# One decoder block on one core: planner and scheduler replaced by source order, timed pieces and one paced list of conditioning and gate

## The chip, the cores and the metric

The kernel runs on one core of a Trainium2 chip. The metric is the device time of one execution in microseconds: the median of three runs before the change is 1742.32 us (1741.33 to 1743.38).

## The reference

One layer on x of 256 tokens by 4096 channels, all float32:

```python
mod = silu(c) @ w_ada + b_ada               # c: 4096 values, w_ada: 4096 x 12288
shift, scale, gate = split(mod, 3)
h = rmsnorm(x, norm_g) * (1 + scale) + shift
p = h @ w_in                                # 4096 x 14336: a_b, a_c, a_x, a_z, b_v, b_g, b_z
y_a = a_b * conv3(a_c * a_x) * silu(a_z)    # causal depthwise, along the tokens
u = conv31(b_v * sigmoid(b_g)) + conv_b_b
y_b = silu(layernorm(u)) * silu(b_z)
out = rmsnorm(x + gate * (concat(y_a, y_b) @ w_out), final_g)
```

## The kernel before

**Products.** The activations are the stationary operand (128 channels by 128 tokens), the weights stream as 512 columns. Each float32 operand is split in a high part and a low remainder, so one block of 128 channels by 512 columns takes six matmuls (`products`, L142): three for each half of the tokens. This text calls these six a *unit*. `w_in` has 28 column tiles of 32 units (896 units), `w_out` 8 of 32 (256), 1152 in all. Weights come two units at a time, 512 KB (`load_w`, L131): a DMA on SP's queue, the high part by a cast on ScalarE (L138, tile w_h), the low part by a subtraction on VectorE (L139, tile w_l). A *step* of the program is two units; there are three buffers of each part.

**Blocks.** The 32 channel blocks are worked in six passes over all 28 column tiles (`BLOCKS`, L31), so that the first pass needs only the first blocks' activations. Between passes a tile's sum is taken out of PSUM (tile acc, L446) and put back (L438), both on ScalarE. In the last pass the tiles finish one after another, and the work on the heads starts: 31 taps of the long convolution for four groups of heads (L350: four products on ScalarE, L351: one sum on VectorE, 120 such pairs), the short convolution (`silu_gate_A`), the transposes of both on TensorE, then the layer norm (`norm_B`) and the gates of y_b while the first half of `w_out` is multiplied.

**Conditioning.** scale, shift and gate are 96 columns of 128 values, each a product of a 128 x 4096 slice of `w_ada` with silu(c), summed along the row by VectorE (`ada_steps`, L179, sum on L189): four *pieces* of 1024 columns (512 KB) for each. A channel block needs the eight pieces of its scale and shift before its activations can be made (`make_h`, L233). The 128 pieces of gate are needed only by the end of the layer.

**Order.** The source puts work at steps: `run_due` (L287) calls what a queue has due at a step; scale and shift pieces get their times from a hull over the first use of each block (L411), the gate pieces are spread evenly over 170 steps from the start of the last pass (L426, `GATE_RUN`). On top of that the tile framework's scheduler orders the instructions of each engine by its own priorities and costs. Within an engine, and on SP's DMA queue, instructions then run strictly in that order. Weights are asked for one step ahead (`AHEAD`). Seven buffers of 512 KB serve weights and pieces alike (`raws`, L92).

Of the kernel before, what the change touches and what calls it, by code (L numbers as in the profile page):

```python
# [16 lines left out]
ALU = mybir.AluOpType  # L17
# [13 lines left out]
BLOCKS = (4, 4, 4, 6, 6, 8)  # L31

EARLY = {0: 12, 1: 10}
KD = 2
AHEAD = 1
LEAD = 2
KEEP = 3
HOLD = 5
ROW = 1024
GATE_RUN = (0, 170)  # L40
A_SPAN = 5

# [42 lines left out]
def decoder_block(ctx: ExitStack, tc: tile.TileContext, x, c, w_mod, w_gate, w_in, w_out, xt, pk, final_g, out):  # L85
    nc = tc.nc
    const = ctx.enter_context(tc.tile_pool(name="const", bufs=1))
    const.tile([P, 420], F32, name="pad")
    big = ctx.enter_context(tc.tile_pool(name="big", bufs=33))
    cbc = ctx.enter_context(tc.tile_pool(name="cbc", bufs=1))  # L90
    dram = ctx.enter_context(tc.tile_pool(name="dram", bufs=1, space=bass.MemoryType.DRAM))
    raws = ctx.enter_context(tc.tile_pool(name="raws", bufs=7))  # L92
    split = ctx.enter_context(tc.tile_pool(name="split", bufs=3))
# [19 lines left out]
    pks = const.tile([P, PK], F32, name="pks")  # L113
    nc.scalar.dma_start(pks, pk)
# [6 lines left out]
    def rsqrt(y, v, t):  # L121

        nc.scalar.activation(out=t, in_=v, func=AF.Sqrt)
        nc.vector.reciprocal(out=y, in_=t)
        nc.vector.tensor_tensor(out=t, in0=y, in1=y, op=ALU.mult)
        nc.vector.tensor_tensor(out=t, in0=t, in1=v, op=ALU.mult)
        nc.vector.tensor_scalar(out=t, in0=t, scalar1=-0.5, scalar2=1.5, op0=ALU.mult, op1=ALU.add)
        nc.vector.tensor_tensor(out=y, in0=y, in1=t, op=ALU.mult)


    def load_w(src, k0, name, keep=False):  # L131
        raw = rawt(f"{name}_r")
        nc.sync.dma_start(raw, src[k0 // KD])
        if keep:
            hi, lo = (bigt(f"{name}_{t}", (P, KD, CT), F32R) for t in "hl")
        else:
            hi, lo = (split.tile([P, KD, CT], F32R, tag=t, name=f"{name}_{t}") for t in "hl")
        nc.scalar.copy(hi, raw)  # L138
        nc.vector.tensor_tensor(out=lo, in0=raw, in1=hi.bitcast(F32), op=ALU.subtract)  # L139
        return hi, lo  # L140

    def products(ps, act, parts, k0, first, last, tokens=range(NS), seeded=False):  # L142

        hi, lo = parts
        for i in range(KD):
            a = act[(k0 + i) // 2]
            f, l = first and i == 0, last and i == KD - 1
            for s in tokens:
                out = ps[s] if isinstance(ps, list) else ps[:, s]
                ah, al = (a[:, (k0 + i) % 2, h, s * P:(s + 1) * P] for h in range(2))  # L150
# [13 lines left out]
    pts = [const.tile([P, 4], F32, name=f"part{i}") for i in range(4)]  # L164
    part_no = itertools.count()
    cB = cbc.tile([P, D], F32, name="cB")
    hT = {}

    def broadcast_c():

        for q in range(D // ROW):
            row = bigt(f"crow{q}", (P, ROW))
            nc.sync.dma_start(row[:1], c[:, q * ROW:(q + 1) * ROW])
            ps = pmm.tile([P, NS, CT], F32, tag="ps", name=f"cps{q}")
            for h in range(2):
                nc.tensor.matmul(ps[:, h], ones[:1], row[:1, h * CT:(h + 1) * CT], start=True, stop=True)  # L176
            nc.scalar.activation(out=cB[:, q * ROW:(q + 1) * ROW], in_=ps, func=AF.Silu)

    def ada_steps(name, srcs, bias, dst):  # L179

        state = {}

        def step(q):
            raw = rawt(f"{name}_{q}", (P, ROW))
            nc.sync.dma_start(raw, srcs[q])
            if q == 0:
                state["part"] = pts[next(part_no) % 4]
            p = state["part"]
            nc.vector.tensor_tensor_reduce(out=raw, in0=raw, in1=cB[:, q * ROW:(q + 1) * ROW], scale=1.0, scalar=p[:, q - 1:q] if q else bias, op0=ALU.mult, op1=ALU.add, accum_out=dst if q == D // ROW - 1 else p[:, q:q + 1])  # L189

        return [lambda q=q: step(q) for q in range(D // ROW)]

    def mod_steps(k):

        def finish():
# [6 lines left out]
        return work + [finish]  # L202
# [12 lines left out]
    def gate_steps():
        work = [f for k in range(KT) for f in ada_steps(f"gate{k}", w_gate[k], pks[:, O_BGATE + k:O_BGATE + k + 1], gateT[:, k:k + 1])]
        return work + [gate_finish]


    plan = [(w_in[e], k) for _, e, k0, k1 in SEGS for k in range(k0, k1, KD)]  # L220
    end_in = len(plan)
    start_last = sum((k1 - k0) // KD for b, _, k0, k1 in SEGS if b < len(BLOCKS) - 1)
    conv_end = end_in + CONV_END
    plan += [(w_out[dt], k0 + k) for k0 in (0, KT // 2) for dt in range(NDT) for k in range(0, KT // 2, KD)]
    loaded = []
    step = 0

    def load_ahead(last):
        while len(loaded) <= min(last, len(plan) - 1):
            src, k = plan[len(loaded)]  # L230
            loaded.append(load_w(src, k, f"w{len(loaded)}", 0 <= len(loaded) - len(plan) + KT // 2 // KD < HOLD))

    def make_h(k0, n):  # L233

        if k0 + n <= 4 * len(kept):
            srcs = [kept[k // 4][:, k % 4:k % 4 + 2] for k in range(k0, k0 + n, 2)]
        else:
            xc = rawt(f"xc{k0}", (P, n, S))
            nc.sync.dma_start(xc, xt[:, k0:k0 + n])
            srcs = [xc[:, q:q + 2] for q in range(0, n, 2)]  # L240
        for q, src in enumerate(srcs):
            nc.vector.tensor_tensor(out=src, in0=src, in1=rstd.unsqueeze(1).broadcast_to([P, 2, S]), op=ALU.mult)
            for i in range(2):
                k = k0 + 2 * q + i
                nc.scalar.activation(out=src[:, i], in_=src[:, i], func=AF.Identity, scale=gscT[:, k:k + 1], bias=modT[:, k:k + 1])
            t = hT[k0 // 2 + q] = bigt(f"hT{k0 // 2 + q}", (P, 2, 2, S), F32R)
            split_act(t, src)


    kept = []  # L250

    def x_stats():

        ps = misc("x_ps", (P, S))
        for ci in range(8):
            xc = bigt(f"xs{ci}", (P, 4, S))
            nc.sync.dma_start(xc, xt[:, 4 * ci:4 * ci + 4])
            sq = xc
            if ci < KEEP:
                kept.append(xc)  # L260
                sq = bigt(f"xq{ci}", (P, 4, S))
            nc.scalar.activation(out=sq, in_=xc, func=AF.Square)
            if ci == 0:
                total = sq
            else:
                nc.vector.tensor_tensor(out=total, in0=total, in1=sq, op=ALU.add)
        for i in range(4):
            nc.tensor.matmul(ps, ones, total[:, i], start=i == 0, stop=i == 3)
        y = const.tile([P, S], F32, name="x_rstd")
        nc.vector.tensor_scalar(out=total[:, 2], in0=ps, scalar1=1.0 / D, scalar2=EPS, op0=ALU.mult, op1=ALU.add)  # L270
        rsqrt(y, total[:, 2], total[:, 3])
        return y

    broadcast_c()
    rstd = x_stats()
    first_steps = [f for k in range(KD) for f in mod_steps(k)]
    for f in first_steps[:-4]:
        f()
    load_ahead(AHEAD)
    for f in first_steps[-4:]:  # L280
        f()
# [341 lines left out]
```

## Time and profile before

| | |
|---|---|
| median of three runs | 1742.32 us |
| profiled execution, its own time | 1744.85 us |
| its span | 1743.0 us |
| TensorE busy | 1644.6 us (94%), 7073 matmuls |
| VectorE busy | 1421.8 us (82%) |
| ScalarE busy | 1163.6 us (67%) |
| DMA | 524.51 MB, mean 301 GB/s |

The busy time of TensorE is no measure of its work here: a matmul's record lasts longer than the distance to the next. What counts is the distance from one product to the next, and where it is longer than in an undisturbed stretch. The stages below are cut at products number 1, 769, 4033, 5377 and 6145 of the 6912 (units 0, 128, 672, 896 and 1024), so that the stretch between two cuts can be compared with the number of its products.

### The profile page before, as it was taken

What the parts mean: (1) busy time and instruction counts of PE and PEld (TensorE: products, weight loads), DVE (VectorE), ACT (ScalarE), POOL (GpSimd) and SP (SyncE); (2) the same over time, 40 slices, a digit from 0 to 9 for tenths busy, and PEclk for the clock granted to TensorE, in tenths of its full rate; (3) what the DMA queues carried; (4) which work ended last, traced back from release to release, by engine and by line L of the source; (5) the groups of instructions that cost most, each with busy time, mean ns of one, the idle gap of its engine ahead of it and who ended that gap; (6) DMA issues with size and microseconds to landing.
All of it is one profiled execution on the core that took longest, in us unless ns stands there. A gap on an engine that the chain in (4) does not pass through costs nothing.

```text
span 1743.0 us, 20848 instructions
## 1 busy us (share of the span) xinstructions
PE 1644.6 (94%) x7073; PEld 1323.9 (76%) x7073; DVE 1421.8 (82%) x1707; ACT 1163.6 (67%) x1558; POOL 1.0 (0%) x8
## 2 busy tenths in 40 slices
PE   4799999999999999999999999989998999999997
PEld 1577788888888888888888777766666777778885
DVE  6887777877777777787776899999999999976675
ACT  4555966577666556566556599998898777464453
POOL 0000000000000000000000000000000000000000
PEclk9999999999999999999999999999999999999999
DMA  8998999999999999999998998868887999679663
GB/s 318 319 363 322 325 328 343 321 335 326 327 317 343 330 322 320 324 342 313 333 326 308 332 304 286 300 220 273 271 266 264 314 314 320 221 273 321 201 201 149
DMA packets 146771, 524.51 MB, mean 301 GB/s; under 512 B 16196, under 2 KB 16228, under 8 KB 146664
## 3 DMA queue, kind: packets, MB, share of 16 engines
q1 hardware_dynamic: 146520, 522.81, 86.1%
q8 instruction: 55, 0.90, 0.2%
q10 hardware_dynamic: 144, 0.37, 0.1%
q14 instruction: 52, 0.43, 0.1%
HBM read 518.91 MB, written 4.21 MB: 300 GB/s over the span
## 4 chain that ended last, share of the span: by engine, by line
PE 63%; DVE 18%; issue 10%; ACT 5%; DMA 4%; DVEq 0%; ACTq 0%
PE ps L152 17%; PE ps L153 17%; PE ps L151 17%; DVE w_l L139 5%; DVE cv L351 5%; DVE gate L189 3%; PE pb L151 3%; PE pb L153 3%; PE pb L152 3%; DMA mod<-in_w_mod 2%; ACT w_h L138 2%; ACT pr L350 1%; DVE mod L189 1%; DMA gate<-in_w_gate 1%; PE cps L176 1%
## 5 line engine op out<-in xcount | busy, mean ns | idle before, releaser
L139 DVE TENSOR_TENSOR w_l<-w_r,w_h 128x1024 fp32r<-128x1024 f32 x576 | 702.7, 1226 | 236.1 <-ACT w_h L138 234.3
L138 ACT CAST w_h<-w_r 128x1024 fp32r<-128x1024 f32 x576 | 600.2, 1048 | 260.1 <-PE ps L153 140.7
L152 PE MATMUL ps<-w_l,hT 128*128 128x512 f32 x1792 | 709.4, 396 | 26.5 <-DVE w_l L139 26.3
L151 PE MATMUL ps<-w_h,hT 128*128 128x512 f32 x1792 | 703.4, 393 | 27.6 <-ACT hT L157 18.1
L153 PE MATMUL ps<-w_h,hT 128*128 128x512 f32 x1792 | 703.6, 393 | 1.1 <-DVE hT L158 1.1
L152 PEld LDWEIGHTS ps<-w_l,hT 128*128 128x128 f32 x1792 | 339.2, 189 | 115.4 <-DVE w_l L139 46.2
L151 PEld LDWEIGHTS ps<-w_h,hT 128*128 128x128 f32 x1792 | 339.5, 190 | 104.0 <-ACT hT L157 19.2
L153 PEld LDWEIGHTS ps<-w_h,hT 128*128 128x128 f32 x1792 | 339.6, 190 | 71.9 <-DVE hT L158 3.2
L446 ACT ACTIVATE acc<-ps 128x1024 f32<-128x1024 f32 x163 | 167.4, 1027 | 223.0 <-PE ps L153 222.6
L189 DVE CUSTOM_DVE_ANT_0 mod<-mod,cB,part 128x1024 f32<-128x1024 f32 x192 | 245.7, 1280 | 26.0 <-DMA mod<-in_w_mod 24.1
L350 ACT ACTIVATE pr<-uT,pks 128x255 f32<-128x255 f32 (+14 forms) x480 | 197.0, 488 | 1.8 <-DVE cv L351 1.6
L351 DVE TENSOR_TENSOR cv<-cv,pr 128x1020 f32<-128x1020 f32 (+14 forms) x120 | 140.3, 1169 | 3.6 <-ACT pr L350 3.4
L438 ACT COPY ps<-acc 128x1024 f32<-128x1024 f32 x135 | 137.0, 1016 | 0.4
L189 DVE CUSTOM_DVE_ANT_0 gate<-gate,cB,part 128x1024 f32<-128x1024 f32 x96 | 124.2, 1294 | 1.6 <-DMA gate<-in_w_gate 1.5
L152 PE MATMUL pa<-w_l,yT 128*128 128x512 f32 x256 | 104.0, 406 | 7.9 <-DVE w_l L139 7.4
L151 PE MATMUL pa<-w_h,yT 128*128 128x512 f32 x256 | 100.3, 394 | 1.8 <-ACT w_h L138 1.8
L153 PE MATMUL pa<-w_h,yT 128*128 128x512 f32 x256 | 100.9, 394 | 0.0
L151 PE MATMUL pb<-w_h,yT 128*128 128x512 f32 x256 | 99.7, 389 | 0.0
L152 PE MATMUL pb<-w_l,yT 128*128 128x512 f32 x256 | 99.6, 389 | 0.0
L153 PE MATMUL pb<-w_h,yT 128*128 128x512 f32 x256 | 99.6, 389 | 0.0
L189 DVE CUSTOM_DVE_ANT_0 mod<-mod,cB,pks 128x1024 f32<-128x1024 f32 x64 | 81.9, 1280 | 12.3 <-DMA mod<-in_w_mod 12.3
L152 PEld LDWEIGHTS pa<-w_l,yT 128*128 128x128 f32 x256 | 48.7, 190 | 27.4 <-DVE w_l L139 17.6
(122 smaller groups left out, 678.5 us busy)
## 6 DMA issues: line engine op xcount, KB each, us to landing
w_r<-in_w_in SPq DMA_DIRECT2D x448, 512.0 KB, 5.0
mod<-in_w_mod SPq DMA_DIRECT2D x256, 512.0 KB, 5.1
gate<-in_w_gate SPq DMA_DIRECT2D x128, 512.0 KB, 4.6
w_r<-in_w_out SPq DMA_DIRECT2D x128, 512.0 KB, 4.6
xs<-in_xt SPq DMA_DIRECT2D x8, 512.0 KB, 10.0
xr<-in_x SPq DMA_DIRECT2D x8, 512.0 KB, 6.7
out<-o SPq DMA_DIRECT2D x16, 256.0 KB, 2.9
xc<-in_xt SPq DMA_DIRECT2D x10, 256.0 KB, 4.6
```

The costliest lines, as they stand in the source:

```text
L138: nc.scalar.copy(hi, raw)
L139: nc.vector.tensor_tensor(out=lo, in0=raw, in1=hi.bitcast(F32), op=ALU.subtract)
L151: nc.tensor.matmul(out, ah, hi[:, i], start=f, stop=False, skip_group_check=seeded)
L152: nc.tensor.matmul(out, ah, lo[:, i], start=False, stop=False, skip_group_check=seeded)
L153: nc.tensor.matmul(out, al, hi[:, i], start=False, stop=l, skip_group_check=seeded)
L176: nc.tensor.matmul(ps[:, h], ones[:1], row[:1, h * CT:(h + 1) * CT], start=True, stop=True)
L189: nc.vector.tensor_tensor_reduce(out=raw, in0=raw, in1=cB[:, q * ROW:(q + 1) * ROW], scale=1.0, scalar=p[:, q - 1:q] if q else bias, op0=A ...
L350: nc.scalar.activation(out=pr[:, j, sh:], in_=u[:, j, :S - sh], func=AF.Copy, scale=cbw[:, 4 * i + j, TAPS - 1 - sh:TAPS - sh])
L351: nc.vector.tensor_tensor(out=o[:, :, sh:], in0=o[:, :, sh:], in1=pr[:, :, sh:], op=ALU.add)
L438: nc.scalar.copy(ps, acc[e])
L446: nc.scalar.activation(out=acc[e], in_=ps, func=AF.Silu if k1 == KT and e >= 24 else AF.Copy)
```

## The change

- `tc.manual_schedule()`: the scheduler no longer orders anything; each engine runs in source order. The work beside the products is cut into one-engine pieces which the source puts at set units (`put`).
- Weights are asked for two steps ahead, in four buffers of their own; conditioning pieces are 2048 columns (1 MB), two for a column, in three buffers of their own.
- One list (`filler`) holds the pieces of scale and shift in the order of their use, and behind them all of gate. `run_due` takes the next one when a running account of VectorE's time and of the DMA's (at `RATE`, 0.385 MB per us) says that it fits, or when it is due.
- The first pass is two blocks; 15 of its tiles do the first block alone (`ALONE`), so one column of conditioning precedes the first product instead of two. The statistics of x are taken from x by ScalarE's row sums (L354) rather than by sums of squares on VectorE.
- In the second half of `w_out` the first half's sum is put back into PSUM by ScalarE (`seed_b`) instead of being added by VectorE. The gate's column goes to DRAM from ScalarE's queue.

```diff
-BLOCKS = (4, 4, 4, 6, 6, 8)
-EARLY = {0: 12, 1: 10}
+BLOCKS = (2, 4, 4, 6, 8, 8)
+ALONE = 15
+EARLY = {1: 14}
-AHEAD = 1
+AHEAD = 2
+ROW = 2048
...
+UNIT = 1.363
+FIRST = 29.0
+RATE = 0.385
+W_LOAD = 0.2622
+ADA_LOAD = 1.0486
+LOW_PART = 0.57
+ADA_SUM = 2.42
+SLACK = 3.0
...
+            if b == 0 and n < ALONE:
+                k1 = 1
...
+    def run_due():
+
+        nonlocal vec, load
+        t = FIRST + UNIT * now
+        while queue and queue[0][0] <= now:
+            _, cost, f = queue.pop(0)
+            vec = max(vec, t - SLACK) + cost
+            f()
+        while filler:
+            due, mb, cost, f = filler[0]
+            if due > now and (max(vec, t - SLACK) + cost > t + UNIT * KD or max(load, t - SLACK) + mb / RATE > t + UNIT):
+                break
+            filler.pop(0)
+            vec = max(vec, t - SLACK) + cost
+            load = max(load, t - SLACK) + mb / RATE
+            f()
...
+    work = [f for k in range(1, KT) for f in mod_steps(k)]
+    gates_due = end_in + KT // 2 * NDT - 20
+    need = [(FIRST_USE[k] - H_DUE, len(work) * k // (KT - 1)) for k in range(1, KT)]
+    work += gate_steps()
...
+    for n, f in enumerate(work):
+        filler.append((float(np.interp(n + 1, [d for _, d in hull], [t for t, _ in hull])), ADA_LOAD, ADA_SUM, f))
...
-    spread(gate_steps(), start_last + GATE_RUN[0], start_last + GATE_RUN[1])
...
-    with tile.TileContext(nc) as tc:
+    with tile.TileContext(nc) as tc, tc.manual_schedule():
```

**What it moves.** VectorE before the first product. Before, the row sums of the conditioning for two channel blocks (ISA, tiles mod) stand between the steps of the reciprocal root of x's mean square (x_rstd):

```order
L124 RECIPROCAL x_rstd<-xq_126 128x256
L189 ISA mod_1_3_204,modT<-mod_1_3_204,cB,part_95 128x1024
L189 ISA modT 128x1
L125 TENSOR_TENSOR xq_126<-x_rstd 128x256
L189 ISA mod_0_0_207,part_96<-mod_0_0_207,cB,pks 128x1024
L189 ISA part_96 128x1
L126 TENSOR_TENSOR xq_126<-xq_126 128x256
L139 TENSOR_TENSOR w_l<-w_r,w_h 128x1024
L127 TENSOR_SCALAR xq_126<-xq_126 128x256
L196 SCALAR_TENSOR_TENSOR gscT<-modT,pks 128x1
L128 TENSOR_TENSOR x_rstd<-x_rstd,xq_126 128x256
L139 TENSOR_TENSOR w_l<-w_r,w_h 128x1024
```

After, with the root already made for one value per token (tiny, yb):

```order
L162 TENSOR_TENSOR tiny<-tiny 128x2
L368 TENSOR_SCALAR yb<-ones,tiny 128x128 x2
L269 ISA mod_1_1_179,modT<-mod_1_1_179,cB,pts 128x2048
L269 ISA modT 128x1
L277 SCALAR_TENSOR_TENSOR gscT<-modT,pks 128x1
L319 TENSOR_TENSOR xc_177<-xc_177,rstd 128x256
L269 ISA mod_0_0_184,pts<-mod_0_0_184,cB,pks 128x2048
L269 ISA pts 128x1
L216 TENSOR_TENSOR w_l<-w_r,w_h 128x512 x3
L269 ISA mod_0_1_205,modT<-mod_0_1_205,cB,pts 128x2048
L269 ISA modT 128x1
L251 TENSOR_TENSOR hT_209<-xc_177,hT_209 128x256
```

One block's four sums of 2048 columns stand there, three half-size low parts between them, and the block's activations (hT) follow at once.

VectorE in the last pass, while the third group's convolution runs (cv is its sum, pr a tap, gate a piece of the gate's column). Before:

```order
L189 ISA gate_0_10589,part_94<-gate_0_10589,cB,pks 128x1024
L189 ISA part_94 128x1
L139 TENSOR_TENSOR w_l<-w_r,w_h 128x1024
L351 TENSOR_TENSOR cv_8199<-cv_8199,pr_23_10611 128x4x233
L139 TENSOR_TENSOR w_l<-w_r,w_h 128x1024
L189 ISA gate_1_10635,part_94<-gate_1_10635,cB,part_94 128x1024
L189 ISA part_94 128x1
L351 TENSOR_TENSOR cv_8199<-cv_8199,pr_24_10638 128x4x232
L139 TENSOR_TENSOR w_l<-w_r,w_h 128x1024
L189 ISA gate_2_10662,part_94<-gate_2_10662,cB,part_94 128x1024
L189 ISA part_94 128x1
L139 TENSOR_TENSOR w_l<-w_r,w_h 128x1024
```

After, at the same tap of the same group:

```order
L216 TENSOR_TENSOR w_l<-w_r,w_h 128x1024
L269 ISA gate_0_10303,pts<-gate_0_10303,cB,pks 128x2048
L269 ISA pts 128x1
L216 TENSOR_TENSOR w_l<-w_r,w_h 128x1024
L497 TENSOR_TENSOR cv_8100<-cv_8100,pr_23_10298 128x4x233
L216 TENSOR_TENSOR w_l<-w_r,w_h 128x1024
L497 TENSOR_TENSOR cv_8100<-cv_8100,pr_24_10327 128x4x232
L216 TENSOR_TENSOR w_l<-w_r,w_h 128x1024
L497 TENSOR_TENSOR cv_8100<-cv_8100,pr_25_10351 128x4x231
L216 TENSOR_TENSOR w_l<-w_r,w_h 128x1024
L497 TENSOR_TENSOR cv_8100<-cv_8100,pr_26_10375 128x4x230
L216 TENSOR_TENSOR w_l<-w_r,w_h 128x1024
```

Before, a gate piece stands beside nearly every low part (w_l); after, one of twice the length is left in this stretch, since most of the list has been worked off earlier.

SP's queue in the middle of the third pass (w_r is a weight load, mod a piece). Before:

```order
L133 DMA w_r<-in_w_in 128x1024
L185 DMA mod_0_3_4189<-in_w_mod 128x1024
L133 DMA w_r<-in_w_in 128x1024 x3
L185 DMA mod_1_0_4250<-in_w_mod 128x1024
L133 DMA w_r<-in_w_in 128x1024
L185 DMA mod_1_1_4273<-in_w_mod 128x1024
L133 DMA w_r<-in_w_in 128x1024 x2
L185 DMA mod_1_2_4313<-in_w_mod 128x1024
L133 DMA w_r<-in_w_in 128x1024
```

After:

```order
L210 DMA w_r<-in_w_in 128x1024 x2
L268 DMA mod_1_1_2488<-in_w_mod 128x2048
L210 DMA w_r<-in_w_in 128x1024 x2
L268 DMA mod_0_0_2531<-in_w_mod 128x2048
L210 DMA w_r<-in_w_in 128x1024 x2
L268 DMA mod_0_1_2572<-in_w_mod 128x2048
L210 DMA w_r<-in_w_in 128x1024 x2
L268 DMA mod_1_0_2612<-in_w_mod 128x2048
```

Before, pieces of 512 KB come at about two for three weight loads; after, one of 1 MB follows every second weight load, that is every four units.

## Rows read from the trace of the kernel before

**Rows 1.** By stage: length, busy PE, PEld, DVE, ACT, POOL (counts), PEclk, DMA share, GB/s

```profile
53.70:238.60 184.90, 180.70 (x769) 144.74 (x770) 147.53 (x188) 121.83 (x130) 0.00 (x0) 1.00 0.92 333
238.60:981.80 743.20, 741.61 (x3266) 612.27 (x3265) 563.44 (x685) 466.98 (x490) 0.00 (x0) 1.00 0.92 326
981.80:1357.10 375.30, 340.58 (x1441) 266.60 (x1440) 360.67 (x439) 331.47 (x580) 0.00 (x0) 0.96 0.83 279
1357.10:1556.40 199.30, 189.56 (x810) 148.53 (x808) 191.66 (x221) 140.25 (x233) 0.00 (x0) 0.98 0.83 285
1556.40:1730.80 174.40, 174.37 (x771) 144.12 (x769) 116.89 (x111) 79.24 (x100) 0.00 (x0) 1.00 0.68 229
1730.80:1743.10 12.30, 0.00 (x0) 0.00 (x0) 5.16 (x15) 2.87 (x6) 0.00 (x0) 0.66 0.47 183
```

**Rows 2.** Timeline of TensorE, two products: start, duration, instruction

```profile
1690.26 0.39 PE L153 MATMUL pb<-w_h,yT 128*128 128x512 f32 x1
...
1709.30 0.39 PE L153 MATMUL pb<-w_h,yT 128*128 128x512 f32 x1
```

**Rows 3.** Waits of TensorE, 981.8 to 1357.1: total, times, longest

```profile
PE ps L152 <- DVE w_l L139: 21.2, 27, 2.7
PE ps L151 <- ACT w_h L138: 9.4, 6, 4.0
```

**Rows 4.** Stage 981.8 to 1357.1, tiles acc alone: busy PE, PEld, DVE, ACT

```profile
981.80:1357.10 375.30, 15.00 (x96) 11.65 (x96) 14.42 (x12) 61.09 (x60) 0.96 0.83 279
```

**Rows 5.** Timeline of VectorE in that stage

```profile
1227.09 1.22 DVE L139 TENSOR_TENSOR w_l<-w_r,w_h 128x1024 fp32r<-128x1024 f32 x1
1228.23 1.28 DVE L189 CUSTOM_DVE_ANT_0 gate<-gate,cB,part 128x1024 f32<-128x1024 f32 x1
...
1229.43 1.13 DVE L351 TENSOR_TENSOR cv<-cv,pr 128x932 f32<-128x932 f32 x1
1230.47 1.22 DVE L139 TENSOR_TENSOR w_l<-w_r,w_h 128x1024 fp32r<-128x1024 f32 x1
```

**Rows 6.** The same stage, gate pieces alone: busy DVE

```profile
981.80:1357.10 375.30, 106.80 (x84) 0.96 0.83 279
```

**Rows 7.** Timeline of ScalarE in that stage

```profile
1218.87 1.02 ACT L446 ACTIVATE acc<-ps 128x1024 f32<-128x1024 f32 x1 [0.59 <-PE ps L153]
1219.79 1.04 ACT L138 CAST w_h<-w_r 128x1024 fp32r<-128x1024 f32 x1
1220.72 1.02 ACT L438 COPY ps<-acc 128x1024 f32<-128x1024 f32 x1
...
1222.19 4.68 ACT L350 ACTIVATE pr<-uT,pks 128x235 f32<-128x235 f32 x12
```

**Rows 8.** Timeline, before the first product

```profile
17.12 1.02 ACT L177 ACTIVATE cB<-cps 128x1024 f32<-128x1024 f32 x1 [1.45 <-PE cps L176]
...
19.93 4.83 ACT L262 ACTIVATE xs<-xs 128x1024 f32<-128x1024 f32 x5
...
24.78 1.28 ACT L123 ACT_TABLE_LOAD   x1
...
52.47 0.60 ACT L245 ACTIVATE xs<-xs,modT,gscT 128x256 f32<-128x256 f32 x1 [1.42 <-DVE modT L189]
...
53.78 0.79 PE L151 MATMUL ps<-w_h,hT 128*128 128x512 f32 x1 [16.74 <-ACT hT L157]
```

**Rows 9.** Timeline of VectorE near the end, a one-column step

```profile
1724.42 0.16 DVE L128 TENSOR_TENSOR o_y<-o_y,o_t 128x1 f32<-128x1 f32 x1
```

**Rows 10.** Busy time in three short stretches, columns of rows 1

```profile
8.00:28.00 20.00, 9.08 (x11) 2.99 (x9) 11.25 (x17) 11.91 (x12) 0.00 (x0) 1.00 1.03 420
...
750.00:800.00 50.00, 50.00 (x222) 41.43 (x221) 39.55 (x48) 30.68 (x35) 0.00 (x0) 1.00 0.98 353
757.00:773.00 16.00, 16.00 (x72) 13.24 (x71) 13.02 (x16) 9.51 (x11) 0.00 (x0) 1.00 1.02 409
```

**Rows 11.** The page, DMA issues: count, size of one, us to landing

```profile
w_r<-in_w_in SPq DMA_DIRECT2D x448, 512.0 KB, 5.0
```

More of the change, by code (lines that the diff above doesn't have):

```diff
@@ L142, in products, with table, rsqrt_steps, root @@
-    def products(ps, act, parts, k0, first, last, tokens=range(NS), seeded=False):
+    def table(func):
+        nc.scalar.activation(out=dummy, in_=ones[:, 0:1], func=func)
+    def rsqrt_steps(y, v, t):
+        def root():
+            nc.scalar.activation(out=t, in_=v, func=AF.Sqrt)
+        def rest():
+            nc.vector.reciprocal(out=y, in_=t)
+            nc.vector.tensor_tensor(out=t, in0=y, in1=y, op=ALU.mult)
+            nc.vector.tensor_tensor(out=t, in0=t, in1=v, op=ALU.mult)
+            nc.vector.tensor_scalar(out=t, in0=t, scalar1=-0.5, scalar2=1.5, op0=ALU.mult, op1=ALU.add)
+            nc.vector.tensor_tensor(out=y, in0=y, in1=t, op=ALU.mult)
+        return root, rest
@@ new lines, in decoder_block, with put @@
+    plan = [(w_in[e], k, n) for _, e, k0, k1 in SEGS for k, n in _steps(k0, k1)]
+    end_in = sum(n for _, _, n in plan)
+    start_last = sum(k1 - k0 for b, _, k0, k1 in SEGS if b < len(BLOCKS) - 1)
+    conv_end = end_in + CONV_END
+    plan += [(w_out[dt], k0 + k, KD) for k0 in (0, KT // 2) for dt in range(NDT) for k in range(0, KT // 2, KD)]
+    loaded = []
+    step = 0
+    now = 0
+    queue = []
+    filler = []
+    vec = load = 0.0
+    def put(t, f, cost=0.0):
+        queue.append((t, cost, f))
+        queue.sort(key=lambda e: e[0])
@@ new lines, in spread @@
+    def spread(work, start, end, cost=0.0):
+        for i, f in enumerate(work):
+            put(start + i * (end - start) / len(work), f, cost)
+    def run_due():
[13 more added lines that the diff above has]
+            f()
@@ new lines, in load_w @@
+    def load_w(i):
+        nonlocal vec, load
+        src, k, n = plan[i]
+        raw = raws.tile([P, KD, CT], F32, tag="r", name=f"w{i}_r")
+        part = slice(k % KD, k % KD + n)
+        nc.sync.dma_start(raw[:, part], src[k // KD][:, part])
+        if 0 <= i - len(plan) + KT // 2 // KD < HOLD:
+            hi, lo = (bigt(f"w{i}_{t}", (P, KD, CT), F32R) for t in "hl")
+        else:
+            hi, lo = (split.tile([P, KD, CT], F32R, tag=t, name=f"w{i}_{t}") for t in "hl")
+        nc.scalar.copy(hi[:, part], raw[:, part])
+        nc.vector.tensor_tensor(out=lo[:, part], in0=raw[:, part], in1=hi[:, part].bitcast(F32), op=ALU.subtract)
+        t = FIRST + UNIT * now
+        vec = max(vec, t - SLACK) + LOW_PART * n
+        load = max(load, t - SLACK) + W_LOAD * n / RATE
+        return hi, lo
@@ L144, in products, with next_w, advance @@
+    def next_w():
+        while len(loaded) <= min(step + AHEAD, len(plan) - 1):
+            loaded.append(load_w(len(loaded)))
+        return loaded[step]
+    def advance():
+        nonlocal step, now
+        now += plan[step][2]
+        step += 1
+    def products(ps, act, parts, k0, n, first, last, tokens=range(NS), seeded=False):
         hi, lo = parts
-        for i in range(KD):
-            a = act[(k0 + i) // 2]
-            f, l = first and i == 0, last and i == KD - 1
+        for k in range(k0, k0 + n):
+            f, l = first and k == k0, last and k == k0 + n - 1
@@ L215, in gate_steps @@
[L215 to L247, printed above, removed]
@@ L250, in decoder_block @@
[L250 to L277, printed above, removed]
-        f()
-    load_ahead(AHEAD)
-    for f in first_steps[-4:]:
-        f()
-    make_h(0, KD)
-    queue = []
-    def run_due(step):
-        while queue and queue[0][0] <= step:
-            queue.pop(0)[1]()
-    def spread(work, start, end):
-        queue.extend((start + i * (end - start) / len(work), f) for i, f in enumerate(work))
-        queue.sort(key=lambda t: t[0])
@@ new lines, in decoder_block @@
+    crow = [bigt(f"crow{q}", (P, 1024)) for q in range(4)]
+    for q in range(4):
+        nc.sync.dma_start(crow[q][:1], c[:, q * 1024:(q + 1) * 1024])
+    xn = []
+    for q in range(4):
+        for s in range(NS):
+            t = bigt(f"xn{q}_{s}", (P, 1024))
+            nc.sync.dma_start(t, xv[:, s, q * 1024:(q + 1) * 1024])
+            xn.append(t)
+    sums = const.tile([P, NS, 8], F32, name="sums")
+    table(AF.Silu)
+    for q in range(4):
+        ps = pst(f"cps{q}")
+        for h in range(2):
+            nc.tensor.matmul(ps[:, h], ones[:1], crow[q][:1, h * CT:(h + 1) * CT], start=True, stop=True)
+        nc.scalar.activation(out=cB[:, q * 1024:(q + 1) * 1024], in_=ps, func=AF.Silu)
+        for i in ((), (0, 1), (2, 3, 4), (5, 6, 7))[q]:
+            nc.scalar.activation(out=xn[i], in_=xn[i], func=AF.Square, accum_out=sums[:, i % 2, i // 2:i // 2 + 1])
@@ new lines, in decoder_block @@
+    table(AF.Sqrt)
+    tiny = const.tile([P, 3, NS], F32, name="tiny")
+    v, y, t = (tiny[:, i] for i in range(3))
+    root, rest = rsqrt_steps(y, v, t)
+    first_mod = mod_steps(0)
+    first_h = h_steps([0])
+    nc.vector.tensor_reduce(out=v, in_=sums[:, :, :4], axis=mybir.AxisListType.X, op=ALU.add)
+    nc.vector.tensor_scalar(out=v, in0=v, scalar1=1.0 / D, scalar2=EPS, op0=ALU.mult, op1=ALU.add)
+    root()
+    first_mod[0]()
+    rest()
+    yb = bigt("yb", (P, NS, P))
+    for s in range(NS):
+        nc.vector.tensor_scalar(out=yb[:, s], in0=ones, scalar1=y[:, s:s + 1], scalar2=None, op0=ALU.mult)
@@ new lines, in decoder_block @@
+    rstd = const.tile([P, S], F32, name="rstd")
+    ps = misc("rstd_ps", (P, S))
+    for s in range(NS):
+        nc.tensor.matmul(ps[:, s * P:(s + 1) * P], yb[:, s], ident, start=True, stop=True)
+    nc.scalar.copy(rstd, ps)
+    table(AF.Silu)
+    first_h[0][0]()
+    first_mod[1]()
+    first_h[1][0]()
+    first_mod[2]()
+    next_w()
+    first_mod[3]()
+    for f, _ in first_h[2:]:
+        f()
+    vec = load = FIRST - SLACK
+    work = [f for k in range(1, KT) for f in mod_steps(k)]
@@ L520, in ahead @@
         def ahead():
-            nc.scalar.activation(out=dummy, in_=ones[:, 0:1], func=AF.Sqrt)
+            table(AF.Sqrt)
             nc.vector.tensor_tensor(out=o, in0=o, in1=g, op=ALU.mult)
```

473 lines of the change are left out of this document (276 added, 197 removed).

## The prediction

> **What bounds the kernel now.** I read the busy times by stage first [rows 1], then the distance of two products [rows 2], then the waits of TensorE in the stage that loses most [rows 3], and last the timelines of the engines it waits for.
>
> A product costs 0.2267 us where nothing disturbs: between two equal ones 84 products apart lie 19.04 us [rows 2]. A unit is then 1.360 us, and 1152 units are 1566.9 us. The span holds 53.7 us ahead of the first product, 1677.1 us from there to the last, and 12.3 us of tail. The stages [rows 1] show where the 110 us beyond the products lie: units 0 to 128 take 184.9 us for 174.1 of products, units 128 to 672 take 743.2 for 739.8, units 672 to 896 (the last pass) 375.3 for 304.6, units 896 to 1024 199.3 for 174.1, and the last 128 units 174.4. Two thirds of the loss is the last pass. The reader is to see in its row that VectorE is busy 360.7 of 375.3 us, and in the next 191.7 of 199.3: there VectorE sets the time, and the stage takes 4% more than its busy time in both. The waits say the same: TensorE waits for low parts most often, then for high parts [rows 3]; the granted clock is 0.96, so some products also ran at 1.2 GHz. Of the 70.7 us lost, 15.0 are the transposes of the heads, work that stays [rows 4].
>
> **The last pass, units 672 to 896.** On VectorE a low part holds the engine 1.14 us until the next instruction, a gate piece 1.20, a tap's sum 1.04 [rows 5]. 84 gate pieces stand in this pass [rows 6], 100.8 us. After the change, by the order of the changed program, 18 pieces of twice the length are left in these units, and 3 in the next 128. Such a piece of 2048 columns is nowhere in the trace. It can't cost more than two of 1024, 2.40 us, nor less than one, 1.20. I take 2.3: one piece of 1024, and as much again as a low part of 1024 columns takes. VectorE's sum becomes 360.7 - 100.8 + 41.4 = 301 us.
>
> ScalarE keeps its work: 112 casts and 56 takes and seeds at 0.93 us, 84 taps at 4.68/3 = 1.56 us [rows 7]: 104 + 52 + 131 = 287, and some 24 for copies of transposed heads, 311 us. TensorE needs 304.6 + 15.0 = 320. So the floor goes from VectorE to TensorE, with ScalarE at 97% of it and VectorE at 94%. Each step's cast must wait for the buffer that TensorE frees two steps before it is used; cast and low part take 2.07 us of those 5.44, so each engine may be some 3 us late. At a change of tile ScalarE has 0.93 + 0.92 + 1.56 = 3.4 us to do in a step of 2.72, in two steps running: this fits, barely. With the 4% of both stages above on 320 it is 333; three engines so close together make me take 335. The bounds are 320 (nothing waits) and 375 (ScalarE takes VectorE's place).
>
> **Units 896 to 1024.** VectorE loses 44 pieces (128 spread over 340 units, 84 of them gone) or 53 us and gains 3 x 2.3: 191.7 - 53 + 7 = 146. TensorE has 174.1 + 5 for 32 more transposes (0.156 us each [rows 4]) + 2 for the means, 181, and is the bound. The steps of the layer norm, now one engine each at set units, keep their chain; I take 184, bounds 181 and 199.3. The cover is VectorE's spare time: filled up again, the old 199.3 returns.
>
> **The start.** The chain to the first product at 53.78 goes through seven sums of squares on VectorE, two blocks' conditioning (16 sums) and a root over 256 columns. After: ScalarE does the squares beside the broadcast of c, three of them ahead of the last slice at 17.12, three behind; at 1.1 us each with the row sum (0.97 in the row of five without it) they end at 22.2; a table load of 1.28 us and a one-column root follow to 23.9 [rows 8]. VectorE from 22.2: four pieces at 2.3, three half low parts at 0.6 (half of 1.14), some ten small ones at 0.2 (0.16 [rows 9]) and two of 128 to 256 columns at 0.35 make 13.7 us, to 35.9. ScalarE's product by channel, 0.60 [rows 8], and the high part, 0.4: first product at 37. The 8 MB asked for by then take 20 us at 420 GB/s [rows 10] and are not late. Bounds: 34 if the pieces overlap, 42 if a dozen handovers cost 0.4 us each. Against 53.7 the gain is 17.
>
> **Units 0 to 128.** Now this part is thinner on cover. The first 15 tiles do one unit each: by the order VectorE has 14 half low parts (8.4), 6 pieces (13.8) and 1.6 of others for 20.4 us of products, 3.4 too much; ScalarE has a half cast and a take per unit, 1.4 us against 1.36. Before, 10.8 us were lost here, partly to the clock after the long idle time. I expect as much: 185, bounds 178 and 195.
>
> **Units 128 to 672, and the DMA.** A weight load is 0.524 MB [rows 11], a piece 1.049. The list puts one piece behind each second weight load: 2.10 MB per four units, 5.44 us, 386 GB/s from unit 32 to about 704, where before 326 to 333 were asked for [rows 1]. VectorE has 2 x 1.14 + 2.3 = 4.6 us in those 5.44. If the DMA delivers, TensorE runs through: I take 741 for 739.8 of products. It delivered 420 GB/s at the start and 409 in a stretch with all engines at work [rows 10], so 386 is 92 to 94% of what is shown.
>
> The Trainium skill (page "DMA: Bandwidth & Descriptors", section "Specifications") puts the limit that HBM sets for one core at about 358 GB/s, and by it the change would ask for more than there is. By that rule the 353 MB of units 32 to 704 would take an estimated 986 us instead of 914, and the whole about 1740. The two fast stretches [rows 10] do not agree with it.
>
> **Other edits.** Seven sums leave VectorE in the last 128 units, seven seeds join ScalarE, both idle there by a third or more [rows 1]: nothing, 174.4. The tail is the same chain: 12.3. A weight buffer or a piece buffer that is late holds all that is behind it on SP's one queue; four and three of them hold 5.2 MB, 13 us of asking, which covers the 5.0 us to landing [rows 11].
>
> **Sum.** 37 + 185 + 741 + 335 + 184 + 174.4 + 12.3 = 1668.7 us of span. The profiled execution's own time is 1.85 above its span and the median of the runs 2.5 below that: 1668 us.
>
> **Rivals.**
> - *ScalarE takes VectorE's place in the last pass.* For it: its busy record there was 331.5 us [rows 1], more than TensorE's 320, and its work is not lightened. Against it: back to back its instructions need 311. The stage stays at 375: 1708.
> - *The DMA is the bound.* In units 32 to 704 the list asks for 353 MB in 914 us. For it: a stretch of 50 us had the DMA busy for 0.98 of the time at only 353 GB/s [rows 10]. At that rate they take 1000 us, and since the order is fixed, weights behind a late piece stop TensorE: +86, 1754, slower. It decides from 357 GB/s down; between that and 386 the time lies between 1668 and 1742, 1708 at 370. Against it: 409 and 420.
> - *Nothing waits.* All stages at their floors, 37 + 175 + 740 + 320 + 181 + 174.4 + 12.3: 1639.
> - *The start gains nothing*, because the thin first tiles lose what the earlier product wins: 1685.
>
> **How the numbers follow.** The forecast, with the start's rival as its upper side, 0.60, its own range 1652 to 1690; ScalarE 0.17; a DMA short of the asking but faster than before 0.08; a DMA that makes it slower 0.08; nothing waits 0.07. The range from 1648 to 1716 leaves out the slow DMA, half of the partial one, most of the floor case and a part of ScalarE's. A difference of 0.2%, 3.5 us, is about what a measurement of this kernel can tell: faster 0.91, same 0.01, slower 0.08.
>
> **What would show it.** First product at 37 (34 to 42). From unit 128 to 672 no waits of TensorE and 380 to 390 GB/s; waits of VectorE for pieces and of ScalarE for weights there would speak for the DMA. In the last pass VectorE busy near 300 us and TensorE's waits split between low and high parts, 335 us in all; waits for high parts that keep 375 would speak for ScalarE. A piece of 2048 columns at 2.3 us. What would make the prediction wrong as a whole is an engine held in its order by one late transfer: then the stages before the last pass, clean today, lose time.

## The result, and the profile after

The changed kernel takes 1815.04 us (median of four runs, 1813.71 to 1817.72), the one before 1742.40 beside it (1741.33 to 1743.38): 1.0419 times as long, 95% interval 1.0401 to 1.0437. The forecast was 1668.

The busy time by stage of the kernel after, columns as in [rows 1], cut at its own first product and units 128, 672, 896 and 1024:

```profile
0.00:36.40 36.40, 15.21 (x20) 6.08 (x20) 13.00 (x23) 19.75 (x33) 0.99 (x8) 1.00 0.88 327
36.40:235.90 199.50, 189.14 (x768) 146.81 (x769) 157.41 (x159) 141.13 (x162) 0.00 (x0) 0.98 0.91 343
235.90:1047.10 811.20, 784.07 (x3266) 625.89 (x3264) 641.82 (x584) 453.87 (x470) 0.00 (x0) 0.97 0.94 353
1047.10:1410.60 363.50, 338.51 (x1441) 268.04 (x1442) 302.08 (x303) 318.45 (x557) 0.00 (x0) 0.97 0.65 216
1410.60:1606.90 196.30, 186.79 (x799) 149.55 (x797) 151.31 (x138) 149.65 (x251) 0.00 (x0) 0.98 0.65 203
1606.90:1802.90 196.00, 188.43 (x782) 150.97 (x780) 112.71 (x111) 85.55 (x109) 0.00 (x0) 0.95 0.61 197
1802.90:1815.90 13.00, 0.30 (x2) 0.00 (x0) 5.16 (x15) 2.87 (x6) 0.00 (x0) 0.61 0.49 185
```

The first product comes at 36.4 us, 17 earlier, and VectorE's work in the last pass fell from 360.7 [rows 1] to 302.1 us: both as intended. But units 128 to 672, clean before at 743.2, take 811.2, and the last 128 units 196.0 for 174.4. Two rows of the timeline of TensorE in that last stretch, 84 products apart as in [rows 2], show the first cause:

```profile
1758.93 0.39 PE L244 MATMUL pb<-w_h,yT 128*128 128x512 f32 x1
1778.61 0.39 PE L244 MATMUL pb<-w_h,yT 128*128 128x512 f32 x1
```

19.68 us in place of 19.04: a product that waits for nothing costs 0.2343 us, not 0.2267. Over the whole run the mean of the undisturbed distances (0.215 to 0.25 us) is 0.2342 against 0.2272, and 6912 products make 48 us of it. The clock is not the reason. In 50 us at a granted clock of 1.00, with TensorE busy throughout, the kernel after does 215 matmuls, that before 222 [rows 10]:

```profile
900.00:950.00 50.00, 50.00 (x215) 40.22 (x214) 41.11 (x35) 27.23 (x28) 0.00 (x0) 1.00 0.99 373
```

The second cause is in the waits of TensorE (total us, times, longest):

```profile
PE ps L244 <- DVE hT L251: 43.3, 16, 4.8
PE psZ L575 <- DVE cv L578: 16.5, 5, 3.7
PE ps L242 <- ACT hT L248: 11.6, 3, 9.2
...
PE ps L242 <- ACT ps L593: 6.7, 11, 1.8
...
PE ps L243 <- DVE w_l L216: 0.3, 1, 0.3
```

The low parts of weights, which came first in [rows 3], are gone from the list. In their place stand the low part of h, 16 times, and the buffer of the transposed gate (psZ), 5 times. One of the 16, at unit 284, in the timeline of the engines:

```profile
475.46 0.40 PE L242 MATMUL ps<-w_h,hT 128*128 128x512 f32 x1
475.66 1.05 ACT L215 CAST w_h<-w_r 128x1024 fp32r<-128x1024 f32 x1 [5.32 <-PE ps L244]
475.70 0.39 PE L243 MATMUL ps<-w_l,hT 128*128 128x512 f32 x1
...
476.74 1.23 DVE L216 TENSOR_TENSOR w_l<-w_r,w_h 128x1024 fp32r<-128x1024 f32 x1 [2.79 <-ACT w_h L215]
477.88 0.69 DVE L251 TENSOR_TENSOR hT<-xc,hT 128x512 fp32r<-128x512 f32 x1
478.00 0.33 SPq L210 DMA_DIRECT2D w_r<-in_w_in  x1
478.62 0.79 PE L244 MATMUL ps<-w_h,hT 128*128 128x512 f32 x1 [2.53 <-DVE hT L251]
479.22 0.63 PE L242 MATMUL ps<-w_h,hT 128*128 128x512 f32 x1
479.64 0.63 PE L243 MATMUL ps<-w_l,hT 128*128 128x512 f32 x1
```

It reads as a circle through three engines. ScalarE's cast is that of the weights two steps on; it waits for a buffer, which TensorE gives back as the step before ends (475.66). VectorE's low part of those weights waits for the cast, and behind it in VectorE's order stands the low part of the new h. It is put one unit ahead of its use (L400; `H_LEAD`, L51, last entry 1), which with steps of two units is the very step of its use. TensorE's third product needs it and stands 2.53 us. The products behind are 0.43 us apart, and the granted clock is 0.50 there, the level of 1.2 GHz (columns as in [rows 1]):

```profile
478.60:482.00 3.40, 3.38 (x8) 2.70 (x9) 0.00 (x0) 0.00 (x0) 0.00 (x0) 0.50 0.53 154
```

Such products number 157 in the whole run, 65 before.

### The profile page after: what moved, and what is told of

The parts are those of the page before. It is cut to its first block, busy times and chain, and to the rows that moved or that the text cites. A ratio compares the mean times of both kernels' runs of the same rounds, so it can differ in the third digit from the quotient of the medians.

```text
span 1815.9 us, 20052 instructions
## 1 busy us (share of the span) xinstructions
PE 1702.5 (94%) x7069; PEld 1347.3 (74%) x7069; DVE 1383.5 (76%) x1329; ACT 1171.3 (64%) x1587; POOL 1.0 (0%) x8
## 5 line engine op out<-in xcount | busy, mean ns | idle before, releaser
L216 DVE TENSOR_TENSOR w_l<-w_r,w_h 128x1024 fp32r<-128x1024 f32 (+1 forms) x591 | 705.5, 1196 | 388.1 <-ACT w_h L215 387.1
L215 ACT CAST w_h<-w_r 128x1024 fp32r<-128x1024 f32 (+1 forms) x591 | 606.0, 1026 | 599.1 <-PE ps L244 428.1
L244 PE MATMUL ps<-w_h,hT 128*128 128x512 f32 x1792 | 724.9, 405 | 43.3 <-DVE hT L251 43.3
L242 PE MATMUL ps<-w_h,hT 128*128 128x512 f32 x1792 | 725.8, 405 | 19.9 <-ACT hT L248 11.6
L243 PE MATMUL ps<-w_l,hT 128*128 128x512 f32 x1792 | 721.2, 402 | 0.5 <-DVE w_l L216 0.3
L244 PEld LDWEIGHTS ps<-w_h,hT 128*128 128x128 f32 x1792 | 345.2, 193 | 134.0 <-DVE hT L251 50.6
L242 PEld LDWEIGHTS ps<-w_h,hT 128*128 128x128 f32 x1792 | 345.5, 193 | 111.1 <-ACT hT L248 13.5
L269 DVE CUSTOM_DVE_ANT_0 mod<-mod,cB,pts 128x2048 f32<-128x2048 f32 x64 | 150.2, 2347 | 1.9 <-DMA mod<-in_w_mod 1.9
L269 DVE CUSTOM_DVE_ANT_0 mod<-mod,cB,pks 128x2048 f32<-128x2048 f32 x64 | 150.2, 2346 | 0.7 <-DMA mod<-in_w_mod 0.7
L593 ACT COPY ps<-acc 128x1024 f32<-128x1024 f32 x135 | 136.4, 1010 | 0.0
L242 PE MATMUL pb<-w_h,yT 128*128 128x512 f32 x256 | 104.3, 407 | 0.0
L244 PE MATMUL pb<-w_h,yT 128*128 128x512 f32 x256 | 103.4, 404 | 0.0
L269 DVE CUSTOM_DVE_ANT_0 gate<-gate,cB,pts 128x2048 f32<-128x2048 f32 x32 | 75.1, 2346 | 0.0
L269 DVE CUSTOM_DVE_ANT_0 gate<-gate,cB,pks 128x2048 f32<-128x2048 f32 x32 | 75.1, 2346 | 0.0
```

Of the source, the lines that this page charges most:

```text
L215: nc.scalar.copy(hi[:, part], raw[:, part])
L216: nc.vector.tensor_tensor(out=lo[:, part], in0=raw[:, part], in1=hi[:, part].bitcast(F32), op=ALU.subtract)
L242: nc.tensor.matmul(out, ah, hi[:, i], start=f, stop=False, skip_group_check=seeded)
L243: nc.tensor.matmul(out, ah, lo[:, i], start=False, stop=False, skip_group_check=seeded)
L244: nc.tensor.matmul(out, al, hi[:, i], start=False, stop=l, skip_group_check=seeded)
L593: nc.scalar.copy(ps, acc[e])
```

## The experiments

Addresses below are bytes within a partition, from the kernels' own allocation. Before, the pool with h, y and the accumulators begins at 12288 and the split weights at 192512, both multiples of 4096. In the changed kernel the split weights begin at 4096 and the pool of h at 32096. The `pad` of 420 floats (1680 bytes) that had put the pool of h on 4096 went with the change.

**1. The pool of h at a multiple of 128.**

```diff
     rstd = const.tile([P, S], F32, name="rstd")
+    const.tile([P, 8], F32, name="pad")
```

> The changed kernel with 32 bytes more of constants per partition, so that h, y, the accumulators and the kept weights begin at multiples of 128 bytes and not 96 above one; nothing else moves. Theory (the place of the stationary operand in SBUF sets the distance of two products): undisturbed products fall from 0.2344 to 0.2267 us, 32 undisturbed units from 45.0 to 43.5, the whole by 6912 x 0.0077 = 53 us to about 1762. Rival (the distance comes from the fixed order, the waits or the transfers beside the products): it stays at 0.2344 and the time at 1815.

Measured: 1804.83 us (ratio to before 1.0349, 1.0334 to 1.0365). The mean distance fell only to 0.2325; the two rows 84 apart are 19.60 us apart:

```profile
1745.94 0.40 PE L244 MATMUL pb<-w_h,yT 128*128 128x512 f32 x1
1765.54 0.40 PE L244 MATMUL pb<-w_h,yT 128*128 128x512 f32 x1
```

So the place matters, but 128 is not the grid that counts. Neither theory had the number right.

**2. The low part of h one step earlier.**

```diff
-H_LEAD = (9, 6, 4, 2, 1)
+H_LEAD = (9, 6, 4, 2, 2)
```

> The changed kernel with the low part of each new pair of h due two units before its use in place of one, that is in the step ahead of its use and not in the same step, where it stands behind the low part of the next weights. Theory (each new pair costs a cast, a low part of weights and its own low part, about 2.9 us, and the products at 1.2 GHz behind it): the 16 waits for hT L251, 43 us, go to a few us, and with a part of the 20 us of half-clock products the time falls to 1750 to 1775. Rival (VectorE is too full there, so the wait moves to a weight's low part): waits of the same sum under another name, 1800 to 1815.

Measured: 1759.05 us (1.0091, 1.0076 to 1.0106), 56.0 less than the changed kernel. The wait is down to 6.7 us, no other grew by more than 3.2 us, and 65 products are left at 0.43 us; units 128 to 672 in the second row:

```profile
PE ps L244 <- DVE hT L251: 6.7, 6, 1.7
```

```profile
231.60:1003.30 771.70, 766.13 (x3265) 614.54 (x3264) 639.84 (x583) 454.82 (x471) 0.00 (x0) 1.00 0.98 370
```

The rival falls: VectorE had the time, the order was wrong. The 771.7 us are 764.4 of products at 0.2342 and 7 of waits.

**3 and 4. One operand of the kernel before moved by 32 bytes.**

```diff
-    const.tile([P, 420], F32, name="pad")
+    const.tile([P, 412], F32, name="pad")
     big = ctx.enter_context(tc.tile_pool(name="big", bufs=33))
+    gap = ctx.enter_context(tc.tile_pool(name="gap", bufs=1))
+    gap.tile([P, 8], F32, name="gap8")
```

> The kernel before with h, y and the accumulators moved by 32 bytes (96 above a multiple of 128, as in the changed kernel), the split weights and all other large buffers where they were. Theory (the stationary operand's place): products go from 0.2267 to about 0.2344 us; units 128 to 672 from 743 to about 768 and the time from 1742 to 1775 to 1795. Rival (the moving operand's place, or the order): stays at 1742.

In the other, the same gap stands ahead of the pool of split weights, and the pad stays.

> The kernel before with the split weights alone moved by 32 bytes, so that the moving operand of the products begins 32 above a multiple of 128. Theory of the stationary operand: no change, products at 0.2267, 1742. Rival (any operand off the grid costs the same): 0.2344 and 1775 to 1795.

Measured: 1773.16 us (1.0166, 1.0149 to 1.0183) and 1769.96 (1.0151, 1.0134 to 1.0168), with a mean distance of 0.2332 in both, a little less than either theory had for a misplaced operand. The theory that only the stationary operand's place counts falls; but both kernels have the pool of h 32 bytes below the weights modulo 256, and the same distance.

**5 and 6. Both operands moved together, and one by 512 bytes.**

```diff
-    const.tile([P, 420], F32, name="pad")
+    const.tile([P, 412], F32, name="pad")
```

> The kernel before with all large buffers, h, the split weights and the rest, moved together by 32 bytes. One theory (what counts is where the two operands lie against each other, modulo some power of two): products stay at 0.2267 us and the time at 1742. The other (each operand counts by itself against a grid): 0.233 us or more, since both are off, and 1770 to 1800.

The other has a pad of 548 and a gap of 896 floats behind the pool of h.

> The kernel before with h, y and the accumulators moved by 512 bytes, the split weights at multiples of 4096 as they were. If a grid of 512 bytes or less is what counts: 0.2267 us, 1742. If the place against the moving operand counts modulo more than 512, or the grid is coarser: 0.231 to 0.234 us, 1765 to 1775.

Single runs: 1747.86 and 1743.84 us, mean distance 0.2272 in both, the value of before. What counts is the place of the two operands against each other.

The trace of the changed kernel shows the same without any edit. The weights of the last tile's first ten units are kept in the pool of h (`HOLD`, L38; L212), so there both operands lie a multiple of 4096 apart; the six units behind take theirs from the split weights again. For the first half of the tokens, the first of 30 products of the one kind, the first of 18 of the other, and the last of these:

```profile
1780.95 0.39 PE L242 MATMUL pb<-w_h,yT 128*128 128x512 f32 x1
...
1787.80 0.40 PE L242 MATMUL pb<-w_h,yT 128*128 128x512 f32 x1
...
1791.77 0.39 PE L244 MATMUL pb<-w_h,yT 128*128 128x512 f32 x1
```

The first distance is 6.85/30 = 0.228 us, the second 3.97/17 = 0.234, some 7 us apart in one execution, both at a granted clock of 1.00; the second half of the tokens repeats it (0.2275 and 0.2339).

**7. The changed kernel with both pools 64 below a multiple of 4096.** In experiments 7 to 12 the earlier low part of experiment 2 stands too.

```diff
-    first.tile([P, 16], F32, name="filler")
...
     rstd = const.tile([P, S], F32, name="rstd")
+    const.tile([P, 168], F32, name="pad")
```

> The changed kernel with the low part of h one step earlier, and with the split weights and the pool of h both 64 bytes below a multiple of 4096 (the filler gone, 672 bytes of constants added). If the place of the operands against each other counts: 0.2267 us, 6912 x 0.0075 = 52 us less than with the earlier low part alone, 1705 to 1712. If each counts against a grid of more than 64 bytes: 0.232 to 0.234, 1750 to 1759.

Measured: 1719.81 us (0.9860, 0.9838 to 0.9883), 39.2 less than experiment 2, not 52. The distance is back (0.2270; 19.04 us for 84), and units 128 to 672 run at the old speed:

```profile
1662.11 0.39 PE L243 MATMUL pb<-w_h,yT 128*128 128x512 f32 x1
1681.15 0.39 PE L243 MATMUL pb<-w_h,yT 128*128 128x512 f32 x1
```

```profile
227.30:975.30 748.00, 742.13 (x3266) 612.35 (x3266) 640.01 (x583) 455.31 (x471) 0.00 (x0) 1.00 1.00 382
```

Products take 49.7 us less in sum; the time between first and last product that is neither products nor half clock grew by 9.8 us, from 79.0 to 88.8, most of it in the last pass. That the other engines have less time beside each step is the likely reason, not one that was tested; the wait for ScalarE's seeds (ps, L593) grew from 6.6 to 10.0.

**8. The last gate spread.** Without the edit of experiment 7.

```diff
-CONV_END = 86
+CONV_END = 78
-NORM_AT = 88
+NORM_AT = 80
...
-            t = end_in + NORM_AT + NORM_STEP * (18 + i + 0.5 * h)
+            t = end_in + NORM_AT + NORM_STEP * (18 + 2 * i + h)
```

> The changed kernel with the low part of h one step earlier, and with the end of the convolution and the layer norm 8 units earlier and the eight half blocks of the last gate two units apart instead of one (theory: transposes one unit apart need the PSUM buffer that the gating two steps on gives back, so TensorE stands 16 us and its products run at 1.2 GHz behind it, some 30 us between units 1008 and 1040; spread out, 25 to 28 of them go: 1731 to 1736). Rival: the taps packed closer into the last pass cost what is won, 1750 to 1759.

Measured: 1736.89 us (0.9957, 0.9942 to 0.9972), 22.2 less than experiment 2 (just short of the 25 to 28 that were expected); the last 128 units fell from 196.0 to 179.8. The wait in experiment 2, and here:

```profile
PE psZ L575 <- DVE cv L578: 16.0, 5, 3.7
PE psZ L575 <- DVE cv L578: 2.1, 2, 1.6
```

The edit also moves the convolution's end and the layer norm, and the two were not tried apart. The named wait is 13.9 us shorter and the half-clock products cost 6.9 less (12.5 to 5.6), together 20.8 of the 22.2.

**9. All three.**

> The changed kernel with all three edits: the low part of h one step earlier, the last gate spread and 8 units earlier, both operand pools 64 bytes below a multiple of 4096. If the three costs are separate, the savings add: 1719.8 less the 22.2 us that the spread gate brought (1759.1 to 1736.9), 1698. If the faster products only turn into waits for VectorE and ScalarE: 1710 to 1720.

Measured: 1704.10 us (median of five, 1698.77 to 1705.13), ratio 0.9765 (0.9746 to 0.9784). It is faster than both kernels and 6 above the sum, between the two theories; the profiled execution took 1701.64. Its stages, from unit 0 to 1152:

```profile
35.50:228.10 192.60, 184.45 (x769) 145.97 (x770) 157.14 (x159) 141.34 (x162) 0.00 (x0) 0.98 0.94 356
228.10:975.80 747.70, 742.11 (x3266) 612.14 (x3265) 639.70 (x583) 455.69 (x471) 0.00 (x0) 1.00 0.99 382
975.80:1323.30 347.50, 326.30 (x1442) 262.57 (x1441) 300.25 (x303) 319.69 (x566) 0.00 (x0) 0.99 0.66 221
1323.30:1509.80 186.50, 180.80 (x806) 147.83 (x804) 156.02 (x145) 148.06 (x246) 0.00 (x0) 1.00 0.69 223
1509.80:1686.80 177.00, 176.45 (x772) 145.65 (x772) 109.83 (x106) 84.52 (x107) 0.00 (x0) 0.99 0.67 218
```

All waits of TensorE in the third of them, the last pass, 20.9 us (psU and psA are the transposes of finished heads):

```profile
PE psU L465 <- DVE acc L459: 5.7, 3, 2.5
PE ps L241 <- ACT ps L593: 4.8, 7, 1.2
PE psA L424 <- DVE acc L417: 4.1, 4, 2.1
PE psA L425 <- DVE acc L418: 3.2, 4, 0.8
PE ps L242 <- DVE w_l L215: 1.8, 4, 0.9
PE ps L243 <- DVE hT L250: 1.3, 1, 1.3
```

**10. All three, and the transposes of finished heads one step later.**

```diff
-        t = now + 2
-        put(t, gates, 2.3)
+        t = now + 4
+        put(now + 2, gates, 2.3)
...
-            put(now + 5, lambda h=h: turn(h))
-            put(now + 5.1 + h, lambda h=h: keep(h))
-        put(now + 8, tap)
-        conv_start = conv_start or now + 10
+            put(now + 7, lambda h=h: turn(h))
+            put(now + 7.1 + h, lambda h=h: keep(h))
+        put(now + 10, tap)
+        conv_start = conv_start or now + 12
...
-            t = max(now + 10, conv_start + i * w)
+            t = max(now + 12, conv_start + i * w)
```

> As combined, with the transposes of finished heads two units later, one step behind the product of heads that they read and not the same step (psU, psA: TensorE waits 11 us for them). If those waits are of the same kind as the low part's: 6 to 10 us less than combined, about 1690. Rival (ScalarE and VectorE are full in the last pass and the wait only moves): within 3 us of combined.

Measured: 1697.73 us (1695.84 to 1701.63), ratio 0.9737 (0.9720 to 0.9755). The ranges of the two overlap by 2.9 us, so the 6.4 between the medians is likely, not settled; the traces put it in the last pass, 341.2 us for 347.5. The waits of the transposes for the heads' products (psU, and psA on acc), 13.0 us in that pass, are gone. In part they have moved: the wait for ScalarE's seeds is 4.8 in that pass in experiment 9 and 10.9 here, and psA waits 3.6 for the short convolution that gives its buffer back (yfA, L436). So both theories hold in part. What the expectation says of the step is wrong: the source puts the product of heads two units behind a tile's end and the transposes five (L442 to L446, L478, L480), which with steps of two units is two steps on, three here, and not the same step. The product still comes late because VectorE runs behind: in experiment 9 one that was put at unit 770 starts at 1134.3 us, though TensorE began that unit at 1127.9, and TensorE stands for it ahead of unit 774. Over the whole run:

```profile
PE ps L241 <- ACT ps L593: 13.1, 16, 3.5
```

**11. All three, with the gate pieces late.**

```diff
-    work += gate_steps()
-    need.append((gates_due, len(work)))
+    gates = gate_steps()
...
+    for n, f in enumerate(gates):
+        put(start_last + 340 * n / len(gates), f, ADA_SUM)
```

> As combined, but the 64 gate pieces of 2048 columns are taken off the list that fills free time and spread over units 672 to 1012, where the kernel before had its 128 of 1024. Theory (the list's early pieces are what frees VectorE in the last pass): VectorE there goes from some 300 to 395 us in units 672 to 896, more than TensorE's, and the time rises by 45 to 70 us to 1745 to 1770. Rival (source order and the fixed times freed the last pass): less than 15 us more.

Measured: 1756.87 us (1.0071, 1.0053 to 1.0090), 52.8 more than experiment 9. The last pass and the stage behind it:

```profile
979.80:1360.90 381.10, 338.96 (x1441) 266.87 (x1440) 356.31 (x353) 322.91 (x568) 0.00 (x0) 0.96 0.75 272
1360.90:1566.70 205.80, 187.38 (x807) 148.98 (x805) 188.50 (x176) 146.52 (x242) 0.00 (x0) 0.98 0.78 279
```

VectorE is at 356.3 us (expected: 395) and the pass at 381.1, the picture of [rows 1]. Source order alone frees nothing there; the list's early pieces do.

**12. The pool of h 256 above a multiple of 512.** Experiment 8 with a pad of 104 floats.

> The changed kernel with the earlier low part and the spread gate (1736.9 without more), split weights at multiples of 4096 and the pool of h 256 above a multiple of 512. The one with 128 above a multiple of 256 had 0.2325 us. If the grid of the relative place is 256: 0.2270 and about 1698. If it is 512: 0.232 to 0.234, 1725 to 1737.

A single run: 1698.81 us, mean distance 0.2270. With experiment 1, where the two places differ by 128 modulo 256, the grid of the relative place is 256 bytes, as far as these distances show (multiples of 256 are fast; 96, 128 and 224 above one are not).

## Why the prediction was wrong

| span, us | forecast | after | all three edits |
|---|---|---|---|
| to the first product | 37 | 36.4 | 35.5 |
| units 0 to 128 | 185 | 199.5 | 192.6 |
| 128 to 672 | 741 | 811.2 | 747.7 |
| 672 to 896 | 335 | 363.5 | 347.5 |
| 896 to 1024 | 184 | 196.3 | 186.5 |
| 1024 to 1152 | 174.4 | 196.0 | 177.0 |
| tail | 12.3 | 13.0 | 13.1 |

- **"A unit is then 1.360 us, and 1152 units are 1566.9 us."** This is the first step that failed. It was read from the kernel before and carried over, though the diff removes the pad and reorders the pools. A place against each other off 256 bytes costs 48 us of products, of which experiment 7 gave 39.2 back in time; shown from both sides (experiments 3 to 7 and 12). Every term between the first product and the last holds a part of it.
- **"From unit 128 to 672 TensorE runs through: I take 741."** This failed too, and cost most: the prediction added up VectorE's work per four units (4.6 of 5.44 us) and didn't ask in which step a low part of h stands, and behind what. That order was in the listing of the changed program. Experiment 2 gives 56.0 us back by a single entry, 39.5 of them in this stage (811.2 to 771.7), so it wasn't VectorE's load. The sign that it named came true, a stage that was clean and lost time, but by another cause: not a late transfer that holds an engine in its order, but a low part put behind an instruction that waits for a buffer.
- **"Seven sums leave VectorE ...: nothing, 174.4", and the layer norm's 184.** The turns of the gate were not looked at by their buffer: two of PSUM, a turn each unit, given back by a piece due one and a half units on. 22.2 us by experiment 8, with the layer norm moved in the same edit, and 15.7 once products were fast (1719.81 to 1704.10).
- **The start** was right: 36.4 for 37, a piece of 2048 columns 2.35 us for 2.3.
- **Units 0 to 128** took 199.5, above the upper bound of 195. Of the 14.5 over the forecast the slower products are 5.4 (768 at 0.2342 for 0.2272), waits for the low part of h in this stretch 5.3. With the three edits it is 192.6, inside the bounds.
- **The last pass** was right in what frees VectorE (302 us for 301, and experiment 11 shows the pieces as the reason) and wrong in what TensorE then waits for. The prediction expected low and high parts of weights; in experiment 9 these are 1.8 of 20.9 us of waits, while the heads' transposes are 13.0 and ScalarE's seeds 4.8. ScalarE, taken at 311 us, was busy for 319.7, as long as TensorE needs (319.6). The 363.5 us of the changed kernel, for 335, hold 9.4 of slower products (1344 of them) and 11.3 of waits for the low part of h besides. With the three edits in it is 347.5: of the 27.9 us over products and transposes the waits are 20.9, products at 1.2 GHz 2.6; some 4 stay open.
- **The rivals.** ScalarE's falls by its own measure (375 in the last pass; it took 363.5, and 341.2 in experiment 10), though its seeds are the longest wait left there. So does the DMA's: with fast products it delivered 382 GB/s for 748 us (experiment 7); TensorE waited 1.0 us for parts of weights in the whole run, and in those 748 us ScalarE's casts waited 284.9 us for TensorE's buffers and 7.7 for transfers. By the limit of 358 GB/s for one core (the Trainium skill, "DMA: Bandwidth & Descriptors", "Specifications") this stage alone could not have taken less than an estimated 798 us, 382 times 748 over 358; the measurement decides against it here. None of the rivals held what happened.

So 111 us of the 147 between forecast and measurement are three omissions, each taken off by an edit. With the three edits the time is 1704, still 36 above the forecast: units 0 to 128 (7.6 us), 128 to 672 (6.7), the last pass (12.5) and small terms. The gain that is left is 40 us against the kernel before beside it (1744.07), little more than half of the 74 that were forecast.

## What to carry to other kernels

When an order is written by hand, follow each engine's list at the first use of every new tile: name the instruction ahead of the one that TensorE needs, and what that one waits for; a sum of busy times doesn't show it. Where a diff moves pools or removes a pad, do not carry a product's duration over: look at the operands' addresses against each other first. A buffer that is given back later than the next one is taken, by the units at which the two are put, is a stall that can be read off the source.

## What was not expected of the hardware

- A 128 by 512 product with its weight load took 0.2270 to 0.2272 us in the kernels whose stationary and moving operand lay equal modulo 256 bytes, 0.2325 at a difference of 128, 0.2332 at one of 224, 0.2342 at one of 96. Moving both by 32 bytes cost nothing. Products at 1.2 GHz are 0.427 us apart in both kernels, so there the place shows no cost. What makes the grid was not tried.
- Stalls cost more than their length: with the low part early, the half-clock products fell from 157 to 65, 30.2 us beyond the normal distance to 12.5.
